# Softmax on one core: stores moved from the load queue to ACT's queue

## The chip, the cores and the metric

The kernel runs on one core of a Trainium2 chip. The metric is the device time of one execution in microseconds; below the span that a profile covers (some 2 us less) is named as such. How far executions agree: 11 runs of the kernel before in one session took 321.05 to 322.64 us.

## The reference

```python
x = np.random.randn(32, 512, 1024).astype(np.float32); temperature = 0.5
scaled  = x / temperature
shifted = scaled - np.max(scaled, axis=-1, keepdims=True)
exp_x   = np.exp(shifted)
return exp_x / np.sum(exp_x, axis=-1, keepdims=True)
```

That is a row softmax over 16384 rows of 1024 floats: 67.11 MB are read from HBM and 67.11 MB are written (the page's HBM line).

## The kernel before

On chip the data lie over 128 partitions (`P = 128` in the kernel). Sixteen transfers of 8 rows a partition (4 MB each) go in, the loads, and sixteen go out, the stores. On chip they live in a ring of 48 rows a partition, six slots of 8. VectorE (DVE in the profile) and ScalarE (ACT) work in groups of 4 rows: maximum and bias on VectorE, exponentials with sums on ScalarE, reciprocal and scaling on VectorE. All loads and all stores are issued by SP, an engine that does nothing else here, into one DMA queue. The page gives the work as a share of 16 DMA engines, and the count of each of the 32 transfers rises in 16 steps, read here as one share of the transfer for each engine. `AHEAD = 2` says how many stores, beyond the older one whose slot a load waits for, are put into the queue ahead of that load.

```python
LOADS = [8] * 16; STORES = [[8]] * 16; RING = 48; GROUP = 4; AHEAD = 2

def _queue(loads, stores, places, ahead):
    ...                                      # cut: flat list of stores
    for i, k in enumerate(loads):
        ...                                  # after = last store of the slot's old data
        while given <= after + ahead and after >= 0 and flat[given][0] < i:
            order.append(("store", given, None)); given += 1
        order.append(("load", i, after))
    order += [("store", n, None) for n in range(given, len(flat))]

# issuing, all on SP
if kind == "load":
    for b in range(after + 1):
        if b > done_to: nc.sync.wait_ge(stored[b], 16)
    nc.sync.dma_start(out=ring[...], in_=dram(xf, ...)).then_inc(loaded[i], 16)
else:
    nc.sync.wait_ge(scaled, part_end[i])
    nc.sync.dma_start(out=dram(of, ...), in_=ring[...]).then_inc(stored[i], 16)

for g in range(len(groups)): exponential(g)          # ACT
for g in range(len(groups) + 1):                     # DVE
    if g < len(groups): maximum(g); shift(g)
    if g > 0: invert(g - 1); divide(g - 1)
```

The order in SP's queue that comes of it is: loads 0 to 5, stores 0, 1, 2, then load 6, store 3, load 7, store 4, and so on in turn to load 15, then stores 12 to 15.

## Time and profile before

The median is 321.85 us (321.15 to 322.12, 3 runs).

| | before |
|---|---|
| span of the profile | 319.9 us |
| DMA data queue, share of the 16 engines' span | 97.9% |
| rate from 80 to 280 us | 431 GB/s |
| VectorE, ScalarE busy | 74%, 47% |
| last store: first and last of the 16 engines land | 313.64 and 318.40 us |

These are lines of the page of the kernel before: span; busy time of the engines; the DMA queues (packets, MB, share of 16 engines' span); issues (KB each, median us from issue to landing).

```profile
span 319.9 us, 568 instructions
...
DVE 235.4 (74%) x224; ACT 149.6 (47%) x257; POOL 0.2 (0%) x4
...
q1 hardware_dynamic: 4608, 134.22, 97.9%
q14 instruction: 4, 0.03, 0.0%
...
DMA 60%; DVE 30%; ACT 3%; issue 0%; SPq 0%
...
ring<-in_x_dram SPq DMA_DIRECT2D x16, 4096.0 KB, 49.0
out_dram<-ring SPq DMA_DIRECT2D x16, 4096.0 KB, 40.5
```

One queue, q1, fills 97.9% of what the engines have to give. A transfer of 4 MB moves in 9.7 us (the spacing of the first five loads), but stands 40 to 49 us between issue and landing: there are always four or so in the queue. The chain of waits, the line with `DMA 60%`, gives VectorE 30%.

The windows view of the kernel before. Its columns are the window and its length in us, busy time and instructions of DVE, ACT and POOL, the granted clock, the DMA share and the GB/s; packets are counted where they start.

```profile
80.00:280.00 200.00, 151.98 (x148) 97.41 (x168) 0.00 (x0) 1.00 1.00 431
...
306.00:310.00 4.00, 0.00 (x0) 0.00 (x0) 0.00 (x0) 1.00 1.02 442
310.00:314.00 4.00, 0.00 (x0) 0.00 (x0) 0.00 (x0) 1.00 0.84 360
314.00:316.00 2.00, 0.00 (x0) 0.00 (x0) 0.00 (x0) 1.00 0.23 98
316.00:318.00 2.00, 0.00 (x0) 0.00 (x0) 0.00 (x0) 1.00 0.08 33
```

The DMA share is 1.00 for 200 us. From 314 us a quarter, then a tenth of the engines still start packets. Some engines are behind the others: of the 16 shares of the last store eleven land within 0.84 us, and five follow 2.1 to 4.8 us after the first.

The waits view of SP's own queue in the kernel before: who waited for whom, us in total, times, longest.

```profile
SPq L171 <- DVE ring L150: 258.9, 16, 29.0
SPq L165 <- DMA out_dram<-ring: 27.6, 9, 9.9
```

SP waits 259 us for VectorE, which looks like a fault and is none: the queue behind it is never empty (DMA share 1.00 from 80 to 280 us).

### The profile page before, as it was taken

The numbers are of one execution on the slowest core, as the hardware profiler recorded it, in microseconds if no ns is written. First come the engines' busy times: TensorE is split into PE (matmuls) and PEld (weight loads), VectorE is DVE, ScalarE is ACT, GpSimd is POOL, SyncE is SP. The second block draws the span as 40 slices with busy tenths as digits, with TensorE's granted clock in tenths as the row PEclk, the third lists the DMA queues.
The fourth block names the chain that finished last, engine by engine and source line by source line (L and its number), as shares of the span: only waits on it lengthen the run. The fifth ranks groups of instructions, "written<-read, shape, count | busy, mean of one in ns | idle before, by whom it ended". The sixth has DMA issues, their size and how long they took to land.

```text
span 319.9 us, 568 instructions
## 1 busy us (share of the span) xinstructions
DVE 235.4 (74%) x224; ACT 149.6 (47%) x257; POOL 0.2 (0%) x4
## 2 busy tenths in 40 slices
DVE  0399999999996966939679495794948949498300
ACT  1076666665555551635516355163553625546000
POOL 0000000000000000000000000000000000000000
DMA  8999999999999999999999999999999999999992
GB/s 328 406 447 443 410 459 406 386 448 438 418 451 406 447 422 430 443 418 434 434 426 443 426 430 431 430 447 422 430 419 434 438 426 434 434 426 443 430 430 115
DMA packets 4612, 134.25 MB, mean 420 GB/s; under 512 B 512, under 2 KB 512, under 8 KB 512
## 3 DMA queue, kind: packets, MB, share of 16 engines
q1 hardware_dynamic: 4608, 134.22, 97.9%
q14 instruction: 4, 0.03, 0.0%
HBM read 67.11 MB, written 67.11 MB: 420 GB/s over the span
## 4 chain that ended last, share of the span: by engine, by line
DMA 60%; DVE 30%; ACT 3%; issue 0%; SPq 0%
DMA ring<-in_x_dram 35%; DMA out_dram<-ring 26%; DVE top L113 18%; DVE ring L150 11%; ACT ring L131 3%; DVE bias L123 1%; DVE recip L144 0%; SPq L219 0%; SPq L156 0%
## 5 line engine op out<-in xcount | busy, mean ns | idle before, releaser
L131 ACT ACTIVATE ring<-ring,bias 128x1024 f32<-128x1024 f32 x128 | 145.4, 1137 | 145.9 <-DVE bias L123 145.9
L113 DVE TENSOR_REDUCE top<-ring 128x4 f32<-128x4096 f32 x32 | 141.3, 4416 | 59.7 <-DMA ring<-in_x_dram 59.7
L150 DVE TENSOR_SCALAR ring<-ring,recip 128x1024 f32<-128x1024 f32 x128 | 87.7, 749 | 1.1
L131 ACT ACTIVATION_READ_ACCUMULATOR ring<-ring,bias 128x1 f32 x128 | 23.9, 187 | 0.0
L144 DVE RECIPROCAL recip<-sums 128x4 f32<-128x4 f32 x32 | 5.5, 171 | 2.0 <-ACT ring L131 2.0
L123 DVE TENSOR_SCALAR bias<-top 128x4 f32<-128x4 f32 x32 | 5.4, 170 | 1.1
L131 ACT ACT_TABLE_LOAD x1 | 1.3, 1283 | 0.9 <-SPq L156 0.9
L205 POOL MEMSET const-bfloat16-1.0<- 128x1 bf16 x1 | 0.1, 101 | 0.0
L205 POOL MEMSET const-uint8-127<- 128x1 uint8 x1 | 0.1, 101 | 0.0
L205 POOL MEMSET const-float32-0.0<- 128x1 f32 x1 | 0.1, 98 | 0.2 <-issue 0.2
L205 POOL MEMSET const-float32-1.0<- 128x1 f32 x1 | 0.1, 98 | 0.0
## 6 DMA issues: line engine op xcount, KB each, us to landing
ring<-in_x_dram SPq DMA_DIRECT2D x16, 4096.0 KB, 49.0
out_dram<-ring SPq DMA_DIRECT2D x16, 4096.0 KB, 40.5
```

What stands on the lines that cost most here:

```text
L113: nc.vector.tensor_reduce(out=top[:, r : r + k], in_=ring[:, s : s + k, :], axis=mybir.AxisListType.X, op=extreme,).then_inc(topped, 1)
L123: nc.vector.tensor_scalar_mul(bias[:, r : r + k], in0=top[:, r : r + k], scalar1=-scale).then_inc(biased, 1)
L131: ins = nc.scalar.activation(ring[:, s + a, :], ring[:, s + a, :], mybir.ActivationFunctionType.Exp, bias=bias[:, r + a : r + a + 1], scal ...
L144: nc.vector.reciprocal(recip[:, r : r + k], sums[:, r : r + k]).then_inc(inverted, 1)
L150: ins = nc.vector.tensor_scalar_mul(ring[:, s + a, :], in0=ring[:, s + a, :], scalar1=recip[:, r + a : r + a + 1])
L205: nc = _bacc.Bacc("TRN2", target_bir_lowering=False, num_devices=1)
```

## The change

The intent is to give each kind of transfer its own queue. SP issues loads alone, each as soon as the old data of its slot is stored. ACT issues each store, in its program behind the exponentials of the next group. The `AHEAD` rule goes.

```diff
-AHEAD = 2
-def _queue(loads, stores, places, ahead): ...
+    def load(i):
+        ...                       # cut: finds the store n of the slot's old data
+                for b in range(free_to + 1, n + 1):
+                    nc.sync.wait_ge(stored[b], 16)
+        nc.sync.dma_start(out=ring[:, s : s + k, :], in_=dram(xf, r, k, i)).then_inc(loaded[i], 16)
+    def store(n):
+        nc.scalar.wait_ge(scaled, part_end[n])
+        nc.scalar.dma_start(out=dram(of, r, k, l), in_=ring[:, s : s + k, :]).then_inc(stored[n], 16)
...
-        for kind, i, after in _queue(LOADS, STORES, places, AHEAD): ...
-        for g in range(len(groups)):
-            exponential(g)
+        for i in range(len(LOADS)):
+            load(i)
+        for g in range(len(groups) + 1):
+            if g < len(groups):
+                exponential(g)
+            for n in range(len(parts)):
+                if part_end[n] == g:
+                    store(n)
```

VectorE's program is untouched.

More of the change, by code (lines that the diff above doesn't have):

```diff
@@ L28, in _places @@
     return places
-def _queue(loads, stores, places, ahead):
-    flat = [(i, n) for i, ks in enumerate(stores) for n in range(len(ks))]
-    last = {i: n for n, (i, _) in enumerate(flat)}
-    order, given = [], 0
-    for i, k in enumerate(loads):
-        over = [
-            b
-            for b in range(i)
-            if places[b] < places[i] + k and places[i] < places[b] + loads[b]
-        ]
-        after = max((last[b] for b in over), default=-1)
-        while given <= after + ahead and after >= 0 and flat[given][0] < i:
-            order.append(("store", given, None))
-            given += 1
-        order.append(("load", i, after))
-    order += [("store", n, None) for n in range(given, len(flat))]
-    return order
 @with_exitstack
@@ L153, in divide @@
         ins.then_inc(scaled, 1)
-    done_to = -1
-    with tc.tile_critical():
-        for kind, i, after in _queue(LOADS, STORES, places, AHEAD):
-            if kind == "load":
-                for b in range(after + 1):
-                    if b > done_to:
-                        nc.sync.wait_ge(stored[b], 16)
-                done_to = max(done_to, after)
-                s, r, k = places[i], first[i], LOADS[i]
-                nc.sync.dma_start(
-                    out=ring[:, s : s + k, :], in_=dram(xf, r, k, i)
-                ).then_inc(loaded[i], 16)
-            else:
-                l, s, r, k = parts[i]
-                nc.sync.wait_ge(scaled, part_end[i])
-                nc.sync.dma_start(
-                    out=dram(of, r, k, l), in_=ring[:, s : s + k, :]
-                ).then_inc(stored[i], 16)
-        for b in range(len(parts)):
-            if b > done_to:
-                nc.sync.wait_ge(stored[b], 16)
-        for g in range(len(groups)):
-            exponential(g)
+    def load(i):
+        nonlocal free_to
+        s, r, k = places[i], first[i], LOADS[i]
+        for n, (l, s1, r1, k1) in enumerate(parts):
+            if l < i and s1 < s + k and s < s1 + k1 and n > free_to:
+                for b in range(free_to + 1, n + 1):
+                    nc.sync.wait_ge(stored[b], 16)
+                free_to = n
+        nc.sync.dma_start(out=ring[:, s : s + k, :], in_=dram(xf, r, k, i)).then_inc(
+            loaded[i], 16
+        )
+    def store(n):
+        l, s, r, k = parts[n]
+        nc.scalar.wait_ge(scaled, part_end[n])
+        nc.scalar.dma_start(out=dram(of, r, k, l), in_=ring[:, s : s + k, :]).then_inc(
+            stored[n], 16
+        )
+    free_to = -1
+    with tc.tile_critical():
+        for i in range(len(LOADS)):
+            load(i)
+        for b in range(free_to + 1, len(parts)):
+            nc.sync.wait_ge(stored[b], 16)
+        for g in range(len(groups) + 1):
[4 more added lines that the diff above has]
+                    store(n)
         for g in range(len(groups) + 1):
```

## The prediction

> **What bounds the kernel now.** The DMA engines. The page's queue part gives the one data queue 97.9% of the 16 engines' span; the windows view shows a DMA share of 1.00 and 427 to 435 GB/s in every stretch from 60 to 300 us. VectorE is busy 74%, ScalarE 47%. Of the 319.9 us span 318.4 pass until the last store lands. A 32 KB packet's record takes 1213 ns in the median, and each engine carries 32 transfers of 8 such packets: 256 x 1.213 = 310.5 us, an estimate of the packets' floor. With about 2 us before data flows and 1.5 us after the last landing, some 314 us of span: no order of transfers can win more than about 6 us, 1.8%.
>
> Where those 6 us are: the landing counts show the first and last of the 16 engines 0.5 us apart for the first load, 1.1 us at load 5, 4.7 us at load 15 and 4.8 us at the last store. Packets over 1260 ns stand at the start, at the first store (58 to 61 us), then near the changes from load to store, every 19.5 us; after 255 us, with the engines far apart, there is none.
>
> **What the change does.** Bytes, VectorE's work and the exponentials stay. The 16 store issues (332 ns each) move from SP to ACT: 5.3 us on an engine idle half the time. Each sits behind the next group's exponentials (4.65 us), while that group's maximum (4.34 us) precedes the divide (2.74 us) on VectorE; so a store is issued about 2 us after it could be, the first at about 34.7 us. SP's 258.9 us of waits for divides vanish, but they held nothing up: 49 and 40 us from issue to landing, against 9.7 us of transfer, mean that the queue was never empty.
>
> What truly changes: the first store no longer stands behind six loads. From 35 us both queues hold work[...]. Each stream then takes about 19.4 us per 4 MB, the sum as before. Estimates: the first store lands near 55 us (72.7 before), the last load near 276 us (279.7 before); stores are issued some 17 us, loads some 30 us before their turn, so neither queue runs dry. At the end store 14 is free 9 us and store 15 20 us after the last load, and a backlog of 3.6 stores (35 us) covers both.[...]
>
> What is left is whether mixed packets go as fast as stretches of one kind. As the present lag stops growing once engines are apart, I expect a small gain from the 4.8 us, or none.
>
> **Predicted**: 320.0 us, range 316.5 to 326. Chances: faster by over 2% 0.04, within 2% 0.86, slower by over 2% 0.10.
>
> **What would show it.** Two data queues whose shares sum to 97 to 99%; DMA share 1.00 in the windows from 40 to 300 us; the first store landing near 55 us, about 20 us from issue; loads landing 19.4 us apart until near 276 us; engine busy times unchanged; no new idle at the end.
>
> **What would make it wrong.** Packets of 1.3 us or more all through the mixed stretch (reads and writes hindering each other): 5% on 240 us is +12 us. Unequal sharing, so that stores starve and the end has a bubble, or loads starve VectorE. Engines drifting further apart, each load then waiting for the slowest engine's store.

The forecast's sum came to 320.0 us, 321.85 us before less some 1.9 us of the 4.8 us lag. The 19.4 us per 4 MB, twice the 9.7 us of a transfer in the kernel before, is an estimate that assumes equal sharing, and so are the landings near 55 and 276 us.

## The result, and the profile after

The changed kernel takes 318.74 us (318.59 to 318.77, 4 runs), the kernel before 321.99 us in the same session (321.15 to 322.59, 4 runs). The ratio is 0.990, 95% interval 0.9877 to 0.9923: within 2%, yet clearly faster by 1%. A ratio here is the mean time of one kernel's fast runs over that of the other's of the same rounds, so it is not quite the ratio of the medians.

The page of the changed kernel, the same lines:

```profile
span 317.0 us, 568 instructions
...
DVE 235.5 (74%) x224; ACT 149.6 (47%) x257; POOL 0.2 (0%) x4
...
q1 hardware_dynamic: 2304, 67.11, 49.6%
q10 hardware_dynamic: 2304, 67.11, 49.0%
q14 instruction: 4, 0.03, 0.0%
...
ring<-in_x_dram SPq DMA_DIRECT2D x16, 4096.0 KB, 49.9
out_dram<-ring ACTq DMA_DIRECT2D x16, 4096.0 KB, 38.9
```

Two data queues now share the engines almost evenly. Engine work is the same to 0.1 us.

The windows view of the changed kernel, the same windows:

```profile
80.00:280.00 200.00, 151.95 (x147) 97.14 (x167) 0.00 (x0) 1.00 1.00 433
...
306.00:310.00 4.00, 0.00 (x0) 0.00 (x0) 0.00 (x0) 1.00 1.06 459
310.00:314.00 4.00, 0.00 (x0) 0.00 (x0) 0.00 (x0) 1.00 0.78 336
314.00:316.00 2.00, 0.00 (x0) 0.00 (x0) 0.00 (x0) 1.00 0.00 0
```

After 314 us no packet starts, where before a few engines went on to 318 us. The SP waits of the changed kernel have turned into waits for landings, as harmless as the old ones (DMA share 1.00, 433 GB/s):

```profile
SPq L142 <- DMA out_dram<-ring: 225.1, 10, 53.9
```

In the traces the semaphore of each transfer rises in 16 steps of 1. Read as one step for each DMA engine as its share lands, they tell when the first and the last engine landed; the time between the two is called the lag here. The following table is worked out from those counts (us from the span's start; first engine, last engine, difference).

```
            before                       after
load 0      12.68   13.15   0.47         12.64   13.35   0.71
store 0     71.58   72.66   1.08         55.84   57.84   1.99
load 10    178.12  181.48   3.36        183.57  185.14   1.58
load 15    274.93  279.67   4.74        280.39  282.92   2.53
store 15   313.64  318.40   4.76        313.63  315.50   1.88
```

This table is the result in five lines (one profiled run of each kernel, as for every lag below). The first engine ends at the same time in both kernels, 313.6 us. What differs is how far the last engine lags: 4.76 us against 1.88 us. The difference, 2.9 us, is the whole difference of the two spans (319.9 and 317.0). In the kernel before the lag grows step by step; in the changed kernel the stores' lag is there from store 0 (1.99 us) and does not grow. So the question for the experiments is what makes engines lag in one queue and why two queues avoid it.

A clue lies in single packets. Of the 4096 packets of 32 KB, most have a record of 1213 ns. Over 1260 ns there are 103 before and 55 after. After 70 us, with the start and the first stores past, there are 54 before and 2 after. Nearly all of the 54 come in bunches 19.5 us apart, each where the leading engines turn from a load to a store; in the changed kernel the two left stand beside 8 KB instruction fetches of queue 14.

### The profile page after: what moved, and what is told of

Same layout as the page of the kernel before. It is cut to its first block, busy times and chain, and to the rows that moved or that the text cites. A ratio compares the mean times of both kernels' runs of the same rounds, so it can differ in the third digit from the quotient of the medians.

```text
span 317.0 us, 568 instructions
## 1 busy us (share of the span) xinstructions
DVE 235.5 (74%) x224; ACT 149.6 (47%) x257; POOL 0.2 (0%) x4
## 3 DMA queue, kind: packets, MB, share of 16 engines
q1 hardware_dynamic: 2304, 67.11, 49.6%
## 4 chain that ended last, share of the span: by engine, by line
DMA 57%; DVE 29%; ACT 5%; another core or an unknown queue 4%; issue 0%; SPq 0%
DMA ring<-in_x_dram 35%; DMA out_dram<-ring 22%; DVE top L91 18%; DVE ring L128 10%; ACT ring L109 5%; DVE bias L101 1%; DVE recip L122 0%; SPq L206 0%; SPq L154 0%
## 6 DMA issues: line engine op xcount, KB each, us to landing
out_dram<-ring ACTq DMA_DIRECT2D x16, 4096.0 KB, 38.9
```

## The experiments

Theory A: engines fall behind where one queue turns from load to store (a turn, from here on). Rival B: the same engines are slow all along, or the waits between compute and transfers make them so. Rival C: the gain comes of having a second queue or another issuer, whatever is in it. A side question was whether the place of the stores in ACT's program matters.

### Transfers alone, three orders

These kernels leave the softmax out. Their outputs are wrong, which doesn't matter for the times. Stores all read one slot that is filled once, loads go round the other five slots, and the queue is never empty (with two queues the DMA share is 1.00 to 1.01 from 60 to 300 us). Only the order differs:

```diff
-    ... all of softmax ...
+    def load(q, i):
+        if i >= 5: q.wait_ge(loaded[i - 5], 16)
+        q.dma_start(out=ring[:, s : s + 8, :], in_=dram(xf, i)).then_inc(loaded[i], 16)
+    def store(q, n):
+        if n == 0: q.wait_ge(filled, 1)
+        if n >= 5: q.wait_ge(stored[n - 5], 16)
+        q.dma_start(out=dram(of, n), in_=ring[:, 0:8, :]).then_inc(stored[n], 16)
+# p_blocks   sync: L0 ... L15 S0 ... S15
+# p_turns    sync: L0 S0 L1 S1 ... L15 S15
+# p_two      sync: L0 ... L15      scalar: S0 ... S15
```

> Transfers alone, no softmax (the result is wrong on purpose): one queue, 16 loads, then 16 stores, so one change from load to store. Theory A (engines fall behind where a single queue turns from load to store): the first and last engine of the last store end 2 us apart or less, as in the changed kernel (1.9 us), no packets over 1260 ns but at the start, at the first store and at single instruction fetches; about 318 us. Rival B (the same engines are slower all along, or the waits between compute and transfers make them so): if slower all along, 4 to 5 us apart here as well and about 321 us; if the waits do it, all three transfer-only kernels end alike.

> The same transfers in one queue, load and store in turn: 16 changes from load to store. Theory A: the engines end 4 to 5 us apart, packets over 1260 ns every 19.5 us, about 321 us, that is 2 to 3 us more than with the loads first. Rival B: the same as with the loads first.

> The same transfers, loads in SP's queue and stores in ACT's, nothing else. Theory A: the engines end 2 us apart or less, about 318 us, like the loads-first kernel and like the changed softmax kernel.[...]

Measured, 4 runs each, before 321.65 us:

| kernel | us | ratio, interval | last store: first, last engine | packets over 1260 ns after 70 us |
|---|---|---|---|---|
| loads, then stores | 316.95 | 0.9856 (0.9841 to 0.9870) | 313.06, 313.82 | 0 |
| in turn | 322.00 | 1.0011 (0.9995 to 1.0027) | 313.66, 319.42 | 80 |
| two queues | 317.37 | 0.9869 (0.9852 to 0.9885) | 313.59, 314.11 | 0 |

The end of the loads-first kernel, in the windows view (DVE and POOL, then clock, DMA share, GB/s):

```profile
310.00:314.00 4.00, 0.00 (x0) 0.00 (x0) 1.00 0.61 262
314.00:316.00 2.00, 0.00 (x0) 0.00 (x0) 1.00 0.00 0
```

The end of the kernel in turn, the same view:

```profile
310.00:314.00 4.00, 0.00 (x0) 0.00 (x0) 1.00 0.80 344
314.00:316.00 2.00, 0.00 (x0) 0.00 (x0) 1.00 0.38 164
316.00:318.00 2.00, 0.00 (x0) 0.00 (x0) 1.00 0.27 115
```

The end of the kernel with two queues, the same view:

```profile
310.00:314.00 4.00, 0.00 (x0) 0.00 (x0) 1.00 0.74 320
314.00:316.00 2.00, 0.00 (x0) 0.00 (x0) 1.00 0.00 0
```

The transfers alone, in turn, take as long as the whole softmax before, so neither compute nor its waits are needed for the lag; and the same transfers with the loads first hardly lag, so no engine is slow all along. The lag is a matter of the order of transfers, and rival B falls. That the two times are equal is in part chance: in turn there are 16 turns and no instruction fetch during the run, in the kernel before fewer turns and four fetches. Loads first and two queues are 5 us quicker, more than the 2 to 3 us expected: their lags are under 1 us and not 2, and the lag in turn is 5.8 us, over the 4 to 5 us expected. One point doesn't fit theory A neatly: the one turn of the loads-first kernel, at 159 us, cost nothing, though the engines were 0.8 us apart. A turn can cost; it does not always.

### The order of slot reuse in one queue

```diff
-AHEAD = 2
+AHEAD = 0
```

> The kernel before, one queue, with no store given ahead (0 instead of 2): the order of slot reuse alone without the second queue. I expect the queue to run empty at each of the ten loads that wait for a store's landing[...]: about 340 us (332 to 350), DMA share below 0.95 from 80 to 280 us. If it stays within 2% of before, the order by itself costs nothing in one queue either.

It took 355.29 us in one run (before: 321.65 us), over the range that I gave. The windows view of this kernel:

```profile
80.00:280.00 200.00, 145.83 (x141) 92.55 (x159) 0.00 (x0) 1.00 0.92 364
```

The direction was right, the size was not: 34 us more over ten loads are 3.4 us each, where the 340 us expected leave 1.8. From the issue of a load into the empty queue to its landing on the first engine pass 12.7 us in the median of the ten, 3.0 us over the 9.7 us of its packets. A part of these 3.0 us fits theory A: as every engine waits for the last, all sixteen turn to the next store together, and near the end of such a load there are packets over 1260 ns (at 106 us 16 of them, 15.2 us in excess together, about 0.9 us an engine). The rest of the 3.0 us is not explained by these runs. So the order of slot reuse alone takes 355.29 us in one queue, and 318.74 us in the changed kernel with a second queue.

### Fewer turns in the softmax, still one queue

The kernel before, with only the order in SP's queue changed: loads and stores in stretches of w, four or two.

```diff
 def _queue(loads, stores, places, ahead):
-    ...
+    n, order, given = len(loads), [("load", i, -1) for i in range(6)], 0
+    for i in range(6, n):
+        if (i - 6) % w == 0:
+            order += [("store", m, None) for m in range(given, given + w)]
+            given += w
+        order.append(("load", i, i - 6))
+    order += [("store", m, None) for m in range(given, n)]
```

> The softmax kernel before, one queue in SP, but loads and stores in stretches of four: 3 changes from load to store after the first, less often than every 19.5 us (before: 10). Theory A (lag grows where one queue turns from load to store) expects a lag of about 2 us at the last store and 318.5 to 320 us, so most of the change's gain without a second queue. Rival C (the gain comes from having a second queue or another issuer) expects 321.5 to 322.5 us, as before.

> The same in stretches of two: 6 changes from load to store. Theory A: a lag between those of fours and of before, 3 to 4 us, and 319.5 to 321 us. Rival C: 321.5 to 322.5 us.

Measured, 6 runs each, before 321.99 us: fours 319.52 us, ratio 0.9918 (0.9900 to 0.9937); pairs 320.05 us, ratio 0.9937 (0.9919 to 0.9955). Lags at the last store are 2.96 and 2.78 us. The end of the kernel in fours, windows view:

```profile
310.00:314.00 4.00, 0.00 (x0) 0.00 (x0) 0.00 (x0) 1.00 0.84 360
314.00:316.00 2.00, 0.00 (x0) 0.00 (x0) 0.00 (x0) 1.00 0.11 49
316.00:318.00 2.00, 0.00 (x0) 0.00 (x0) 0.00 (x0) 1.00 0.00 0
```

Rival C expected no change and falls: one queue with fewer turns gains 0.8%, where the changed kernel gains 1.0%. Theory A's order (fours, pairs, before) is in the medians, but fours and pairs are not told apart by their intervals, and in the profiled runs their lags stand the other way round by 0.2 us. The lag of fours is over the 2 us expected, and pairs' is under its 3 to 4 us. Part of the lag of fours need not come of turns: 0.9 us arise between loads 4 and 5, on one engine alone (the other fifteen land load 5 within 0.56 us), after an instruction fetch at 56.4 us. Nor does the number of slow packets give the lag: after 70 us there are 7 over 1260 ns in fours and 49 in pairs (54 in the kernel before). Whether they fell on the same engine, as a lag would need by the author's reading, was not shown: the records do not name the engine.

### Two queues that both hold loads and stores

Transfers alone again. In the first kernel both queues turn together; in the second each engine was meant to have a load in one queue and a store in the other all the time. The trace shows that it did not (below).

```diff
+# p_inphase     sync: L0 S0 L2 S2 ... L14 S14    scalar: L1 S1 L3 S3 ... L15 S15
+# p_antiphase   sync: L0 S0 L2 S2 ... L14 S14    scalar: S1 L1 S3 L3 ... S15 L15
```

> Transfers alone (result wrong on purpose), two queues, but each holds loads and stores in turn, in the same phase[...]. Theory A (turning together from load to store costs, a second queue does not cure it) expects the engines 3 to 5 us apart at the end and 319.5 to 322 us. Rival C (a second queue cures it) expects 317 to 318 us, as with loads and stores in queues of their own.

> The same with the second queue starting with a store[...]. Theory A and rival C: 317 to 318 us and the engines 1 us apart or less. If it is slower, turns hurt even while the other queue has the opposite kind.

Measured, 4 runs each, before 321.84 us: in phase 321.07 us, ratio 0.9987 (0.9959 to 1.0016), lag 2.8 us at the last transfer; in antiphase 320.97 us, ratio 0.9975 (0.9957 to 0.9993), lag 4.5 us. The end of the antiphase kernel, windows view:

```profile
314.00:316.00 2.00, 0.00 (x0) 0.00 (x0) 1.00 0.30 131
316.00:318.00 2.00, 0.00 (x0) 0.00 (x0) 1.00 0.04 16
```

In phase went as theory A said in time, with a lag just under the 3 to 5 us expected. Its first engine, too, was late by 1.2 us, at 314.8. Most of that came at the first turn: near 21 us every engine has a packet some 0.8 to 1.2 us too long.

Antiphase I took for a miss, as I had expected 317 to 318 us. But the kernel did not do what it was built for. These are its first issues:

```profile
0.94 0.37 SPq L86 DMA_DIRECT2D ring<-in_x_dram  x1
2.72 6.88 DVE L96 MEMSET ring<- 128x8192 f32 x1 [2.72 <-issue]
9.63 0.35 SPq L93 DMA_DIRECT2D out_dram<-ring  x1
9.63 0.39 ACTq L93 DMA_DIRECT2D out_dram<-ring  x1
```

Both first stores wait for the slot to be filled, till 9.63 us, and by then load 0 has had the engines to itself and is nearly through (in the kernel before it lands from 12.68 us). So stores 0 and 1 run side by side and land on their first engines at 32.9 and 33.0 us, then loads 2 and 1 at 52.2 and 52.4 us, stores 2 and 3 at 72.0 and 72.2 us, and so on to stores 14 and 15 at 304.1 and 304.3 us; load 15 is left over alone. From then on both queues hold the same kind: this is a second in-phase kernel, and its time and lag are what theory A expected of one. It does not test whether engines lag while the two queues hold opposite kinds.

So a second queue alone is no cure, which speaks against rival C: where both queues turn together, the engines lag by 2.8 and 4.5 us at the end (one queue: 4.76 us in the kernel before, 5.8 us in turn). Whether two queues of one kind each help because neither turns, or because each engine always has both kinds at hand, these kernels do not tell apart.

### A second queue for half the stores

The changed kernel, but the even stores go back among the loads in SP's queue.

```diff
         for i in range(len(LOADS)):
+            while i >= 6 and given <= min(i - 6 + 2, i - 1):
+                if given % 2 == 0: store(given, nc.sync)
+                given += 1
             load(i)
+        ...                                   # the last even stores
-                if part_end[n] == g:
-                    store(n)
+                if n % 2 == 1 and part_end[n] == g:
+                    store(n, nc.scalar)
```

> The changed kernel with its second queue kept, but the even stores back among the loads in SP's queue, so that this queue still turns from load to store (7 times after the first); the odd stores stay in ACT's. [...]theory A is now: a turn within one queue costs, whatever the other queue holds. It expects packets over 1260 ns near those turns, engines 2.5 to 4.5 us apart at the last store, and 319.5 to 322 us. Rival C (a second queue is enough) expects 318.4 to 319 us and 2 us apart, as in the changed kernel.

It took 326.21 us (324.10 to 328.91, 6 runs; before 321.52 us), ratio 1.0142 (1.0101 to 1.0183): slower than either kernel and outside what theory A expected. The end of this kernel, windows view:

```profile
300.00:306.00 6.00, 4.12 (x8) 3.88 (x8) 0.00 (x0) 1.00 1.01 437
306.00:308.00 2.00, 0.87 (x2) 0.00 (x0) 0.00 (x0) 1.00 0.89 377
308.00:310.00 2.00, 0.00 (x0) 0.00 (x0) 0.00 (x0) 1.00 0.73 311
```

The profiled run is the fastest of the six (324.10 us). Two things add up in it. First, 191 packets are over 1260 ns (55 in the changed kernel), most in bunches in SP's queue; over all packets the excess over 1213 ns is 5.9 us an engine against 1.7 us. The lag is 9.8 us at store 12 and 3.0 us at store 15, the last one within the 2.5 to 4.5 us expected. But of the 129 slow packets after 70 us, 95 stand where no packet of ACT's queue starts within 1.2 us: that queue was empty at most of the turns. So this kernel, too, shows turns that cost where SP's queue works alone, and not what they cost beside a queue of stores. Second, the order makes the last two loads land 10 us apart (272.4 and 282.1 us) where VectorE needs 14.8 us for each (two groups at 7.4 us). Store 15 was issued at 306.90 us, after the first engine had already landed store 14 at 306.78 us: engines ran dry, as the dip from 306 us shows. The second effect is one of this kernel's order alone and no part of theory A, so the size of the loss decides nothing between A and C. It shows only that a second queue is not enough for a gain.

### Stores issued later

The changed kernel with stores placed one group of exponentials later: all but the last three, or all.

```diff
-                if part_end[n] == g:
+                if min(part_end[n] + (1 if n < 13 else 0), len(groups)) == g:   # mid
+                if min(part_end[n] + 1, len(groups)) == g:                      # all
                     store(n)
```

> The changed kernel with each store but the last three issued one group of exponentials later (some 7 us). Stores are issued some 17 us and more before their turn, so I expect no effect: 318.3 to 319.3 us. If placing the stores behind the exponentials matters, it gets slower by several us.

> The same with every store. Store 14 is then issued near 297 us instead of 290.5, while store 13's last packets run from 292 to 296: a gap of about 4 us at the end, 321.5 to 324 us. If it stays at 318.7, the backlog at the end is larger than I read.

Measured, 4 runs each, before 321.84 us: mid 318.80 us, ratio 0.9909 (0.9893 to 0.9925); all 319.27 us (318.74 to 320.70), ratio 0.9928 (0.9898 to 0.9959). The first was as expected. The second was a miss, for a good reason: in its profile the first store is issued at 37.46 us instead of 33.07 us, and the loads use that time. The last load lands at 278.05 us instead of 282.92 us, and store 14 is issued at 290.14 us, no later than in the changed kernel (290.45 us). Late stores give loads a lead, which comes back at the end. Whether the slightly higher median is real is not settled by these runs.

### More instruction fetches

```diff
+    pad = pool.tile([P, 1024], f32, name="pad")
+        for z in range(1024):
+            nc.gpsimd.memset(pad[:, z : z + 1], 0.0)      # POOL is idle otherwise
```

> The changed kernel with 1024 needless small memsets on the idle POOL, so more instruction fetches. The changed kernel has 4 fetches of 8 KB during the run (queue 14), each beside one slow packet, and ends 1.4 us later than its transfers alone, which have none. If the fetches make that, I expect about 8 more of them, each with a slow packet, and 319 to 322 us, by how far they fall on one engine; the engines further than 1.9 us apart at the end. If fetches cost nothing: 318.7 us.

It took 321.69 us (321.26 to 322.17, 6 runs; before 321.52 us), ratio 0.9995 (0.9978 to 1.0011): the change's gain is gone. The DMA queues of this kernel:

```profile
q1 hardware_dynamic: 2304, 67.11, 49.1%
q10 hardware_dynamic: 2304, 67.11, 48.6%
q14 instruction: 12, 0.10, 0.1%
```

The eight further fetches came as expected, seven about every 5.5 us from 6.5 to 39.4 us and one at 45.7 us. They take little of the engines on average (0.1% in queue 14), and one engine lost much, by its landings. At load 2 fifteen landings stand between 32.08 and 32.69 us, and one at 36.24 us; six fetches lay before it, so some 0.7 us each (an estimate). After the other two, and with both queues at work (19.36 us a transfer in the changed kernel, against 9.71 us alone), the loads' last landings are 10.2 us late. The end, windows view:

```profile
306.00:310.00 4.00, 0.00 (x0) 0.00 (x0) 0.00 (x0) 1.00 0.92 393
310.00:314.00 4.00, 0.00 (x0) 0.00 (x0) 0.00 (x0) 1.00 0.93 401
314.00:316.00 2.00, 0.00 (x0) 0.00 (x0) 0.00 (x0) 1.00 1.18 508
```

The last load counts as landed only at 286.17 us, with its last engine; store 15 is issued 19.7 us later, at 305.90 us, and by then the first engine has landed store 14 (304.65 us). So all engines end late: the first at 316.83 us instead of 313.6.

Fetches are also a part of the 1.4 us between the changed kernel (318.74 us) and its transfers alone (317.37 us, no fetch during the run). Its four fetches stand beside packets 0.53, 0.11, 0.26 and 0.53 us too long. They did not all fall on one engine: when the packets are strung together by time, each starting where one before it ended (a reconstruction, since the records do not name their engine), the first and the last fetch, at 65.4 and 240.5 us, lie on the engine that ends last, the other two on two others. The last store's slowest engine lands 0.8 us after the next one, so without its fetches the kernel would have ended 0.8 us sooner at most (an estimate). The rest of the 1.4 us stays open.

## Why the prediction was right

**The time** (320.0 us, 316.5 to 326; measured 318.74) and the class were right, and for the reason given: bytes and engine work are unchanged, the DMA share stays 1.00, so only the lag and the ends could be won. The bound of about 6 us held: even the loads-first transfers alone, at 316.95 us, are only 5 us below before.

**Equal sharing of the engines.** The prediction assumed it. The trace of the changed kernel has it: while both queues hold work the first engine lands loads 19.36 us apart (67.39, 86.76, 106.12), twice the 9.71 us of the first loads, from 60 to 260 us the two queues move 43.35 and 43.12 MB, and over the run their shares are 49.6 and 49.0%.

**The rate with a second issuer.** The rate from 80 to 280 us went from 431 to 433 GB/s, and fours in one queue came to within 0.8 us of two queues (medians of two sessions). The gain is in the order of kinds, not in the rate.

**Neither queue runs dry:** right. Stores are issued well ahead of their turn (38.9 us from issue to landing in the median, where stores land 19.4 us apart), and issuing them a group later changed nothing (318.80 us).

**The first store** was put near 55 us; it landed from 55.84 to 57.84 us. Right, but with some luck: it was issued at 33.07 us instead of 34.7, and took 22.8 us to its first landing instead of "about 20".

**The last load** was put near 276 us and landed at 282.92 us. The sum, which the prediction does not write out, was mis-sized in its first term: 276 us comes out when data flow from the first moment, 3.58 loads by 34.7 us. With 2 us of start (the first packet starts at 1.94 us) it is 3.37 loads, and the 0.21 that are missing cost 4 us at 19.4 us a load: 280 us, the first engine's 280.39 us. The last 2.5 us are the lag.

**The end.** "A backlog of 3.6 stores (35 us) covers both" was right, with less room than it sounds. Store 15 was issued at 302.64 us, and the first engine landed store 14 at 303.95 us: 1.3 us. The padded and the half-stores kernels lost time just there.

**Stores issued 2 us late** was wrong. This is the timeline of the changed kernel around its first store (start, duration, what):

```profile
32.29 0.75 DVE L128 TENSOR_SCALAR ring<-ring,recip 128x1024 f32<-128x1024 f32 x1
...
32.50 1.13 ACT L109 ACTIVATE ring<-ring,bias 128x1024 f32<-128x1024 f32 x1
32.95 4.41 DVE L91 TENSOR_REDUCE top<-ring 128x4 f32<-128x4096 f32 x1
33.07 0.37 ACTq L149 DMA_DIRECT2D out_dram<-ring  x1
33.54 0.19 ACT L109 ACTIVATION_READ_ACCUMULATOR ring<-ring,bias 128x1 f32 x1
33.63 1.13 ACT L109 ACTIVATE ring<-ring,bias 128x1024 f32<-128x1024 f32 x1
```

VectorE's last scaling instruction for this store starts at 32.29 us and takes 0.75 us, to 33.04 us; the store is issued at 33.07 us, while exponentials that precede it in ACT's program still run, till 34.86 us. The issue did not wait for them. As it had no weight in the sum, nothing else changed.

**The gain's size** ("a small gain from the 4.8 us, or none") was placed at 1.9 us and was 3.3 us in medians. The step that under-read it is the last: "As the present lag stops growing once engines are apart, I expect a small gain". Its premise held. The lag levels off in the kernel before (4.60 us at load 13, 4.76 at store 15) and in turn (5.48 us at load 10, 5.76 at store 15). What does not follow is that little can be won: in two queues the stores' lag is not built up at all. It is 1.99 us at store 0 and 1.88 us at store 15, so 2.9 of the 4.8 us were won. The prediction did not ask how far apart the engines would get in the mixed stream.

What stays open: why a turn delays packets, why some turns (the loads-first kernel's only one at 159 us) cost nothing, and whether two queues help by having no turns or by giving each engine both kinds all the time. A run that really holds the two queues in opposite phase, by starting the second queue half a period later, would test the last. No run here looks inside a DMA engine.

## What to carry to other kernels

When the DMA share is 1.00, look at when the first and the last of the 16 engines finish a transfer: here the first landed the last store at 313.6 us in both kernels and the last at 318.40 and 315.50 us, which was the whole difference, and an average of 98% hides it. Queues that each hold one kind of transfer (a lag of 1.88 us), or a single queue that turns from loads to stores seldom (2.96 us in fours), kept the engines closer together than the kernel before (4.76 us), for 1.0 and 0.8% here; a second queue did not help where both queues turned together (321.07 and 320.97 us, before 321.84). In one queue give stores ahead of the loads that wait (taking that away cost 34 us), and when a program grows, look for instruction fetches: here eight more, after which one of load 2's landings came at 36.24 us and the other fifteen by 32.69, cost 3.0 us (318.74 to 321.69 us, medians of two sessions).
